# Three 256-column matmuls per weight tile in place of a 512- and a 256-column one, in the MLP up projection of a two-layer decoder trunk

## The chip, the cores and the metric

The kernel runs on one core of a Trainium2 chip. The metric is device microseconds of one execution. Before the change three runs gave 2304.35, 2304.24 and 2301.83 us, median 2304.24 us. The profile shown here is of one further execution, which took 2303.22 us.

## The reference, cut to what matters

The trunk has two layers over 256 tokens of width 2048. Each layer normalises, runs an attention mixer, adds it back, normalises again and runs a squared-ReLU MLP of inner width 8192:

```python
D_MODEL = 2048; SEQ = 256; D_FF = 4 * D_MODEL

def sq_relu_mlp(h, w_up, w_down):
    return jnp.square(jax.nn.relu(h @ w_up)) @ w_down

def reference(x, ...):
    h = x
    for layer in range(DEPTH):            # DEPTH = 2
        hn = rms_norm(h, ln_mix_g[layer])
        h = h + mixer(hn, ...)            # layer 0: forgetting + dilated heads, layer 1: sparse attention
        hn = rms_norm(h, ln_mlp_g[layer])
        h = h + sq_relu_mlp(hn, w_mlp_up[layer], w_mlp_down[layer])
    return h
```

The change concerns `h @ w_up` and the squared ReLU behind it.

## The kernel before, in words

**Precision.** Each fp32 operand is kept as two fp32r parts, a high part and the rest (low part). A product is the sum of three partial products: high by high, high by low, low by high. The activations lie transposed in `xT[:, k, part]`: 16 slices k of 128 input columns, and for each slice 256 token columns of the high part (part 0), then 256 of the low part (part 1), next to each other.

**Weights.** SP streams weight pieces of 1 MB from HBM into three `raw` buffers (L227). Half a piece is a unit: 128 by 1024 numbers, that is two k-slices of 512 weight columns. ScalarE copies a unit into one of four `wh` buffers (high part, L235), VectorE subtracts to get `wl` (low part, L236). This `split` is issued three units ahead of the unit's matmuls (L264).

**Two kinds of matmul units.** `a_units` (the projections, the out projections and the MLP down projection) stream the weights: a 128-token slice of the activations is the stationary operand, 512 weight columns move; each partial product is one 512-column matmul (L298 to L300 in a group's first and last unit, L311 in the units between, where successive matmuls alternate between two PSUM banks). `b_units` (the MLP up projection only) stream the activations: a 128-column slice j of the weights is stationary. For each k and each j of 4 there are two matmuls: the high weights against the 512 columns [high part | low part] (L340), and the low weights against the 256 columns of the high part (L337), which add into the first half of the same bank. So one PSUM bank holds one j: its left half high-high plus low-high, its right half high-low.

**Order.** In the first and the last unit of a group the order is one j after the other; in the units between, it goes through the four j for one k-slice and then for the other, each low matmul one step behind (L351 to L357). All matmuls load their own stationary operand (a LDWEIGHTS each, `PEld` in the profile), also where two in a row have the same one, as L298 and L299.

**MLP.** The inner width is done in 8 blocks of 1024 columns; `up_units(b)` makes block b in two groups g of 512 columns (8 units each), `down_units(b)` consumes it. The order is up(0), up(1), down(0), up(2), down(1), ..., up(7), down(6), down(7). A group g of the up projection uses four PSUM banks: bank 3 and banks 0 to 2 for g = 0, banks 4 to 7 for g = 1; the down projection uses banks 2n and 2n+1 for its four column groups n.

**Evacuation.** When a j is done in the last unit, `evac` issues a ScalarE copy of the right half to SBUF (L767), a VectorE add of the left half (L768), and a VectorE (max 0) times itself (L769); a background task then makes the high part on ScalarE (L773) and the low part on VectorE (L774), both into `big`. Background tasks (`bg`) are issued in slots: each `yield` of a unit's generator gives one slot (L265, L266), and `bg.need` issues a task at once if it isn't done. Instructions of each engine run in the order issued.

Of the kernel before, what the change touches and what calls it, by code (L numbers as in the profile page):

```python
# [12 lines left out]
AF = mybir.ActivationFunctionType  # L13
ALU = mybir.AluOpType
AX = mybir.AxisListType

S = 256
# [130 lines left out]
def trunk_kernel(ctx: ExitStack, tc: tile.TileContext, x, w_up, w_down, even_w_in, even_w_out,  # L148
                 odd_w_in, odd_w_out, k_w1, k_w2, v_w1, v_w2, vec, rows, con, rot_in, ident_in, out):
    nc = tc.nc  # L150
# [4 lines left out]
    def sb(name, shape, dt=F32):  # L155
        return pool.tile(shape, dt, name=name)

    bank = [psum.tile([128, 512], F32, name=f"bank{i}") for i in range(8)]
# [5 lines left out]
    xT = sb("xT", [128, KT, 2, S], F32R)  # L164
# [5 lines left out]
    T = [sb(f"t{i}", [128, 1024]) for i in range(10)]  # L170
# [26 lines left out]
    bg = Background()  # L197
# [9 lines left out]
    def weight_chunk(w, k0, nk, segs):  # L207

        width = sum(n for _, n in segs)
        pieces, at = [], 0  # L210
        for c0, n in segs:
            src = w[k0 * 128:(k0 + nk) * 128, c0:c0 + n].rearrange("(k p) c -> p k c", p=128)
            pieces.append((nk, width, at, n, src))
            at += n
        return chunk(pieces)
# [101 lines left out]
    def b_units(w, c0, rhs, evac, banks, pre=None):  # L317


        state = {}  # L320
        for i0 in range(0, KT, 4):
            ci = weight_chunk(w, i0, 4, [(c0, 512)])
            for j0 in (0, 2):
                ks = [i0 + j0, i0 + j0 + 1]

                def gen(u, ks=ks):
                    first, last = ks[0] == 0, ks[-1] == KT - 1
                    if pre:
                        pre(ks)
                    if first:  # L330
                        state["banks"] = banks()
                    h = wh[u % NHL].rearrange("p (k c) -> p k c", c=512)
                    lo = wl[u % NHL].rearrange("p (k c) -> p k c", c=512)
                    def part(j, n, lo_part):
                        o, k = state["banks"][j], ks[n]
                        if lo_part:
                            nc.tensor.matmul(o[:, :S], lo[:, n, j * 128:(j + 1) * 128], rhs(k)[:, :S], start=False,  # L337
                                             stop=last and n == 1)
                        else:
                            nc.tensor.matmul(o, h[:, n, j * 128:(j + 1) * 128], rhs(k), start=first and n == 0, stop=False)  # L340

                    if first or last:
                        for j in range(4):
                            for n in range(2):
                                part(j, n, 0)
                                part(j, n, 1)
                            if last:
                                evac(j, state["banks"][j])
                            yield
                    else:  # L350
                        steps = [(j, n) for n in range(2) for j in range(4)]  # L351
                        for i, (j, n) in enumerate(steps):
                            part(j, n, 0)
                            if i:
                                part(*steps[i - 1], 1)
                            if i == 7:
                                part(j, n, 1)  # L357
                            if i % 2:
                                yield

                units.append((ci, j0 * 512, 1024, gen, True))

    def t_units(w, c0, m, rhs, evac, pre):
# [87 lines left out]

    def xr(k):
        return xT[:, k].rearrange("p a t -> p (a t)")

    rot = {"main": 0, "tp": 0, "s": 0, "sq": 0}

    def rotate(name, of):
        rot[name] += 1
        return of[(rot[name] - 1) % len(of)]
# [4 lines left out]
    class Prep:  # L464
# [7 lines left out]
        def evac(self, hf, ps):  # L472
            r = self.norm.rows()
            if hf == 0 and self.src.name in owner:
                bg.need(owner[self.src.name])
            q = self.src[:, hf * 512:(hf + 1) * 512]
            sq = SQ[hf]
            nc.scalar.activation(q, ps, AF.Copy, scale=r[:, hf:hf + 1])
            nc.scalar.activation(sq, ps, AF.Square, scale=r[:, 2 + hf:3 + hf])
            nc.vector.tensor_reduce(self.ms[:, hf * 4:hf * 4 + 4], sq.rearrange("p (h d) -> p h d", h=4), AX.X, ALU.add)  # L480
            if hf == 1:
                self.task = owner[self.src.name] = bg.spawn(self.rest(), 2)

        def rest(self):
            ms = self.ms
            nc.vector.tensor_scalar(ms, ms, EPS, None, op0=ALU.add)
            nc.gpsimd.tensor_tensor(ms, ms, nhalf, ALU.pow)
            yield 4, "d"
            for hf in range(2):
                q = self.src[:, hf * 512:(hf + 1) * 512].rearrange("p (h d) -> p h d", h=4)  # L490
                f = ms[:, hf * 4:hf * 4 + 4, None].to_broadcast([128, 4, HD])
                nc.vector.tensor_tensor(q, q, f, ALU.mult)
                if self.rope is not None:
                    rope(q, self.rope[0][:, hf], self.rope[1][:, hf], 128)
                if hf == 0:
                    yield 3, "d"
            yield 8
            yield (self.free or (lambda: True)), "t"
            yield from self.turn()
# [127 lines left out]
    heads = {}  # L627
# [65 lines left out]
    for kind, base, h0 in (("fox", 0, 0), ("dil", 4 * FOX_W + 8, 8)):  # L693
        for blk in range(2):
# [16 lines left out]
            if nblk == 1:  # L711
                t_units(W, 4 * FOX_W, 8, xr, evac_fa, n0.need)
# [40 lines left out]
    def mlp(layer, norm, nxt):  # L753
        up, down = w_up[layer], w_down[layer]
        NBLK = DFF // 1024

        def hid(b):
            return big[:, (b % 2) * 8:(b % 2) * 8 + 8]

        def up_units(b):  # L760
            for g in range(2):
                def evac(j, ps, g=g):
                    k = g * 4 + j
                    t, s_, q_ = T[j][:, 0:S], T[j][:, S:2 * S], T[j][:, 2 * S:3 * S]
                    if ("hid", j) in heads:
                        bg.need(heads["hid", j])
                    nc.scalar.activation(t, ps[:, S:], AF.Copy)  # L767
                    nc.vector.tensor_tensor(s_, ps[:, :S], t, ALU.add)  # L768
                    nc.vector.scalar_tensor_tensor(q_, s_, 0.0, s_, op0=ALU.max, op1=ALU.mult)  # L769

                    def rest():
                        d = hid(b)
                        nc.scalar.activation(d[:, k, 0], q_, AF.Copy)  # L773
                        nc.vector.tensor_tensor(d[:, k, 1], q_, d[:, k, 0], ALU.subtract)  # L774
                        yield 2
                    heads["hid", j] = bg.spawn(rest(), 1 + j)
                b_units(up, b * 1024 + g * 512, xr, evac, lambda g=g: bank[4:8] if g else [bank[3]] + [rotate("main", bank[0:3]) for _ in range(3)], norm.need)

        def down_units(b):
            for n in range(NB):  # L780
                bks = (bank[2 * n], bank[2 * n + 1])

                def evac(hf, ps, n=n):
                    if n == 0 and hf == 0 and b == 0:
                        bg.need(norm.rtask)
                    xd = xs[:, hf, n * 512:(n + 1) * 512]
                    nc.vector.scalar_tensor_tensor(xd, ps, norm.r2[:, hf:hf + 1], xd, op0=ALU.mult, op1=ALU.add)  # L787
                    if b < NBLK - 1:
                        return
                    if nxt is not None:  # L790
                        nxt.square(n, hf)
                        if hf == 1:
                            m = 2 * ((n + 3) % 4)
                            nxt.start(n, (bank[m], bank[m + 1]), 4)
                            if n == NB - 1:
                                nxt.rtask = bg.spawn(stats(nxt), 4)
                    else:
                        nc.sync.dma_start(out[hf * 128:(hf + 1) * 128, n * 512:(n + 1) * 512], xd)

                a_units(down, [(n * 512, 512)],  # L800
                        lambda k, part, hf: hid(b)[:, k - 8 * b, part, hf * 128:(hf + 1) * 128],
                        list(range(8 * b, 8 * b + 8)), evac, lambda bks=bks: bks,
                        lambda ks: bg.need(*[heads["hid", j] for j in range(4)]))

        for b in range(NBLK):
            up_units(b)
            if b:
                down_units(b - 1)
        down_units(NBLK - 1)

    def even_ready(ks):
# [287 lines left out]
```

## Time and profile before

| | |
|---|---|
| median of three runs | 2304.24 us (2301.83 to 2304.35) |
| profiled execution, its own time | 2303.22 us |
| its span, first to last instruction | 2301.4 us |
| PE busy | 2285.3 us (99%), 11399 matmuls |
| VectorE busy | 1382.1 us (60%) |
| ScalarE busy | 1086.6 us (47%) |
| granted TensorE clock, mean | 0.999 |
| HBM traffic over the span | 179 GB/s |

How to read it: matmuls are pipelined, so a matmul's own duration is longer than the time until the next one starts; the spacing of starts is what adds up to the span. "Releaser" is what ended an engine's wait. L311 means line 311 of the kernel before; `bank<-xT,wh` names the output, the moving operand and the stationary operand in this order for matmuls. Idle time of an engine that is not the bound costs nothing.

### The profile page before, as it was taken

What the parts mean: (1) busy time and instruction counts of PE and PEld (TensorE: products, weight loads), DVE (VectorE), ACT (ScalarE), POOL (GpSimd) and SP (SyncE); (2) the same over time, 40 slices, a digit from 0 to 9 for tenths busy, and PEclk for the clock granted to TensorE, in tenths of its full rate; (3) what the DMA queues carried; (4) which work ended last, traced back from release to release, by engine and by line L of the source; (5) the groups of instructions that cost most, each with busy time, mean ns of one, the idle gap of its engine ahead of it and who ended that gap; (6) DMA issues with size and microseconds to landing.
All of it is one profiled execution on the core that took longest, in us unless ns stands there. A gap on an engine that the chain in (4) does not pass through costs nothing.

```text
span 2301.4 us, 28635 instructions
## 1 busy us (share of the span) xinstructions
PE 2285.3 (99%) x11399; PEld 1922.5 (84%) x11399; DVE 1382.1 (60%) x2075; ACT 1086.6 (47%) x1573; POOL 30.0 (1%) x28
## 2 busy tenths in 40 slices
PE   8999999999999999999999999999999999999999
PEld 6788888888888888888888888788888888888887
DVE  5565655666566566566654666766666556566564
ACT  5554554544444444444443555555544444444342
POOL 0000000000000000000000000000000000000000
PEclk9999999999999999999999999999999999999999
DMA  6555555555555565565546653335555565555654
GB/s 240 165 165 171 176 165 167 181 192 193 184 198 186 188 196 183 183 201 184 188 148 204 215 165 121 118 110 174 191 186 190 181 199 193 187 193 176 203 195 148
DMA packets 212694, 414.47 MB, mean 180 GB/s; under 512 B 10705, under 2 KB 11985, under 8 KB 212561
## 3 DMA queue, kind: packets, MB, share of 16 engines
q1 hardware_dynamic: 211552, 411.53, 54.9%
q8 instruction: 89, 1.46, 0.3%
q10 hardware_dynamic: 1008, 1.12, 0.1%
q14 instruction: 45, 0.36, 0.0%
HBM read 410.52 MB, written 2.10 MB: 179 GB/s over the span
## 4 chain that ended last, share of the span: by engine, by line
PE 96%; DVE 1%; ACT 1%; DMA 1%; issue 0%; POOL 0%; ACTq 0%; POOLq 0%
PE bank L311 34%; PE bank L340 21%; PE bank L337 11%; PE bank L300 8%; PE bank L298 8%; PE bank L299 8%; PE bank L616 1%; PE bank L588 1%; PE bank L611 1%; DMA raw<-in_even_w_in 1%; PE bank L876 1%; DVE wl L236 1%; PE bank L507 1%; PE bank L617 0%; PE bank L425 0%; PE bank L584 0%
## 5 line engine op out<-in xcount | busy, mean ns | idle before, releaser
L236 DVE TENSOR_TENSOR wl<-raw,wh 128x1024 fp32r<-128x1024 f32 (+1 forms) x772 | 937.9, 1219 | 768.5 <-ACT wh L235 766.3
L235 ACT ACTIVATE wh<-raw 128x1024 fp32r<-128x1024 f32 (+1 forms) x772 | 812.3, 1054 | 864.8 <-PE bank L311 324.1
L340 PE MATMUL bank<-xT,wh 128*128 128x512 f32 x2048 | 707.6, 397 | 0.0
L337 PE MATMUL bank<-xT,wl 128*128 128x256 f32 x2048 | 543.0, 281 | 0.0
L340 PEld LDWEIGHTS bank<-xT,wh 128*128 128x128 f32 x2048 | 371.5, 188 | 75.2
L337 PEld LDWEIGHTS bank<-xT,wl 128*128 128x128 f32 x2048 | 386.6, 189 | 18.5
L311 PE MATMUL bank<-wh,big 128*128 128x512 f32 x1280 | 358.8, 391 | 0.0
L311 PE MATMUL bank<-wh,xT 128*128 128x512 f32 x1156 | 325.6, 395 | 0.8 <-ACT xT L430 0.7
L311 PEld LDWEIGHTS bank<-wh,big 128*128 128x128 f32 x1280 | 239.6, 188 | 49.3 <-DVE big L625 0.2
L298 PE MATMUL bank<-wh,big 128*128 128x512 f32 x640 | 252.8, 395 | 0.0
L311 PEld LDWEIGHTS bank<-wh,xT 128*128 128x128 f32 x1156 | 214.9, 188 | 44.6 <-ACT xT L430 1.3
L300 PE MATMUL bank<-wh,big 128*128 128x512 f32 x640 | 249.5, 390 | 0.0
L299 PE MATMUL bank<-wl,big 128*128 128x512 f32 x640 | 249.2, 389 | 0.0
L311 PE MATMUL bank<-wl,big 128*128 128x512 f32 x640 | 202.8, 393 | 0.0
L311 PE MATMUL bank<-wl,xT 128*128 128x512 f32 x578 | 188.5, 397 | 0.0
L300 PEld LDWEIGHTS bank<-wh,big 128*128 128x128 f32 x640 | 120.1, 188 | 25.7 <-DVE big L625 0.4
L298 PEld LDWEIGHTS bank<-wh,big 128*128 128x128 f32 x640 | 120.4, 188 | 24.4 <-ACT big L624 0.2
L311 PEld LDWEIGHTS bank<-wl,big 128*128 128x128 f32 x640 | 120.2, 188 | 24.5
L299 PEld LDWEIGHTS bank<-wl,big 128*128 128x128 f32 x640 | 120.4, 188 | 23.5
L311 PEld LDWEIGHTS bank<-wl,xT 128*128 128x128 f32 x578 | 108.5, 188 | 22.5 <-DVE wl L236 0.2
L787 DVE SCALAR_TENSOR_TENSOR xs<-bank,r_m,xs 128x512 f32<-128x512 f32 x128 | 89.9, 743 | 7.8 <-PE bank L300 7.8
L773 ACT ACTIVATE big<-t 128x256 fp32r<-128x256 f32 x128 | 52.5, 415 | 81.9 <-DVE t L769 81.9
(179 smaller groups left out, 1454.9 us busy)
## 6 DMA issues: line engine op xcount, KB each, us to landing
raw<-in_w_up SPq DMA_DIRECT2D x128, 1024.0 KB, 5.3
raw<-in_w_down SPq DMA_DIRECT2D x128, 1024.0 KB, 5.1
raw<-in_even_w_in SPq DMA_DIRECT2D x55, 1024.0 KB, 5.1
raw<-in_odd_w_in SPq DMA_DIRECT2D x40, 1024.0 KB, 5.1
raw<-in_even_w_out SPq DMA_DIRECT2D x16, 1024.0 KB, 5.0
raw<-in_odd_w_out SPq DMA_DIRECT2D x16, 1024.0 KB, 5.3
out_x<-xs SPq DMA_DIRECT2D x8, 256.0 KB, 2.5
xs<-in_x SPq DMA_DIRECT2D x3, 512.0 KB, 8.8
```

Of the source, the lines that this page charges most:

```text
L235: nc.scalar.activation(h, r, AF.Copy)
L236: nc.vector.tensor_tensor(lo, r, h, ALU.subtract)
L298: nc.tensor.matmul(o, lhs(k, 0, hf), h[:, n], start=st, stop=False)
L299: nc.tensor.matmul(o, lhs(k, 0, hf), lo[:, n], start=False, stop=False)
L300: nc.tensor.matmul(o, lhs(k, 1, hf), h[:, n], start=False, stop=last and n == len(ks) - 1)
L311: nc.tensor.matmul(bks[hf], lhs(k, part, hf), w_[:, n], start=False, stop=False)
L337: nc.tensor.matmul(o[:, :S], lo[:, n, j * 128:(j + 1) * 128], rhs(k)[:, :S], start=False, stop=last and n == 1)
L340: nc.tensor.matmul(o, h[:, n, j * 128:(j + 1) * 128], rhs(k), start=first and n == 0, stop=False)
L507: nc.tensor.transpose(b[:, i * S + hf * 128:i * S + hf * 128 + 128], self.src[:, hf * 512 + h * 128:hf * 512 + (h + 1) * 128], ident)
L588: nc.tensor.matmul(s[:, 128:384], qT[:, 128:256], kT, start=True, stop=bias is None, skip_group_check=True)
L773: nc.scalar.activation(d[:, k, 0], q_, AF.Copy)
L787: nc.vector.scalar_tensor_tensor(xd, ps, norm.r2[:, hf:hf + 1], xd, op0=ALU.mult, op1=ALU.add)
```

## The change

In `b_units` the 512-column matmul and the 256-column one become three 256-column matmuls that add into the same 256 PSUM columns: high weights by high activations, high weights by low activations, low weights by high activations. Two j share one bank, so a group needs two banks (4 and 5 for g = 0, 6 and 7 for g = 1). All units go one j after the other; there are four yields per unit as before. The evacuation handles two j at a time: ScalarE takes the ReLU of 512 columns straight from PSUM, VectorE squares it, and the background task makes high and low parts of 512 columns. A helper `xr2(k, part)` gives one part of a slice.

```diff
-                    def part(j, n, lo_part):
-                        o, k = state["banks"][j], ks[n]
-                        if lo_part:
-                            nc.tensor.matmul(o[:, :S], lo[:, n, j * 128:(j + 1) * 128], rhs(k)[:, :S], start=False,
-                                             stop=last and n == 1)
-                        else:
-                            nc.tensor.matmul(o, h[:, n, j * 128:(j + 1) * 128], rhs(k), start=first and n == 0, stop=False)
...
+                    for j in range(4):
+                        o = state["banks"][j // 2][:, (j % 2) * S:(j % 2 + 1) * S]
+                        for n, k in enumerate(ks):
+                            hj, lj = h[:, n, j * 128:(j + 1) * 128], lo[:, n, j * 128:(j + 1) * 128]
+
+                            nc.tensor.matmul(o, hj, rhs(k, 0), start=first and n == 0 and j % 2 == 0, stop=False,
+                                             skip_group_check=True)
+                            nc.tensor.matmul(o, hj, rhs(k, 1), start=False, stop=False, skip_group_check=True)
+                            nc.tensor.matmul(o, lj, rhs(k, 0), start=False, stop=last and n == 1, skip_group_check=True)
+                        if last and j % 2:
+                            evac(j // 2, state["banks"][j // 2])
+                        yield
...
-                def evac(j, ps, g=g):
-                    k = g * 4 + j
-                    t, s_, q_ = T[j][:, 0:S], T[j][:, S:2 * S], T[j][:, 2 * S:3 * S]
...
-                    nc.scalar.activation(t, ps[:, S:], AF.Copy)
-                    nc.vector.tensor_tensor(s_, ps[:, :S], t, ALU.add)
-                    nc.vector.scalar_tensor_tensor(q_, s_, 0.0, s_, op0=ALU.max, op1=ALU.mult)
+                def evac(m, ps, g=g):
+                    k, t = g * 4 + 2 * m, T[2 * (g % 2) + m]
+                    r_, q_ = t[:, 0:2 * S], t[:, 2 * S:4 * S]
...
+                    nc.scalar.activation(r_, ps, AF.Relu)
+                    nc.vector.tensor_tensor(q_, r_, r_, ALU.mult)
...
-                        nc.scalar.activation(d[:, k, 0], q_, AF.Copy)
-                        nc.vector.tensor_tensor(d[:, k, 1], q_, d[:, k, 0], ALU.subtract)
+                        d, q2 = hid(b)[:, k:k + 2], q_.rearrange("p (k t) -> p k t", k=2)
+                        nc.scalar.activation(d[:, :, 0], q2, AF.Copy)
+                        nc.vector.tensor_tensor(d[:, :, 1], q2, d[:, :, 0], ALU.subtract)
...
-                b_units(up, b * 1024 + g * 512, xr, evac, lambda g=g: bank[4:8] if g else [bank[3]] + [rotate("main", bank[0:3]) for _ in range(3)], norm.need)
+                b_units(up, b * 1024 + g * 512, xr2, evac, lambda g=g: bank[4 + 2 * g:6 + 2 * g], norm.need)
```

## Rows read from the trace of the kernel before

**Rows 1.** The page's busy time by engine, and the granted clock in 40 slices.
```profile
PE 2285.3 (99%) x11399; PEld 1922.5 (84%) x11399; DVE 1382.1 (60%) x2075; ACT 1086.6 (47%) x1573; POOL 30.0 (1%) x28
...
PEclk9999999999999999999999999999999999999999
```

**Rows 2.** All waits of PE: line waited for, us in total, times, longest us.
```profile
PE bank L425 <- DMA xs<-in_x: 5.4, 2, 4.5
PE bank L985 <- DVE big L625: 2.3, 1, 2.3
...
PE bank L298 <- DVE xT L431: 1.0, 2, 0.8
```

**Rows 3.** Busy time by stretch: one up group, the next down block; us, engines, clock, DMA.
```profile
883.47:906.01 22.54, 22.54 (x130) 19.61 (x129) 14.01 (x21) 10.89 (x16) 0.00 (x0) 1.00 0.57 188
906.01:949.54 43.53, 43.53 (x194) 36.05 (x193) 27.54 (x34) 19.12 (x23) 0.00 (x0) 1.00 0.58 190
```

**Rows 4.** The page's costliest groups: busy us, mean ns of one, idle before.
```profile
L340 PE MATMUL bank<-xT,wh 128*128 128x512 f32 x2048 | 707.6, 397 | 0.0
L337 PE MATMUL bank<-xT,wl 128*128 128x256 f32 x2048 | 543.0, 281 | 0.0
...
L299 PEld LDWEIGHTS bank<-wl,big 128*128 128x128 f32 x640 | 120.4, 188 | 23.5
```

**Rows 5.** Chain of waits: shares of the span by line; pieces at 643 and 1256 us.
```profile
by line: PE bank L311 34.3%; PE bank L340 20.8%; PE bank L337 10.5%; PE bank L300 8.0%; PE bank L298 8.0%; PE bank L299 8.0%; PE bank L616 0.9%; PE bank L588 0.8%; PE bank L611 0.7%; DMA raw<-in_even_w_in 0.7%; PE bank L876 0.6%; DVE wl L23
...
643.11 5.44 PE bank L311 x24
...
1256.26 7.12 PE bank L876 x64
```

**Rows 6.** Timeline of PE, first unit of a group from 506.68 us: start, us, instruction.
```profile
506.68 0.40 PE L340 MATMUL bank<-xT,wh 128*128 128x512 f32 x1
506.91 0.28 PE L337 MATMUL bank<-xT,wl 128*128 128x256 f32 x1
...
509.45 0.40 PE L340 MATMUL bank<-xT,wh 128*128 128x512 f32 x1
```

**Rows 7.** The same view, first unit of the group from 883.47 us.
```profile
883.82 0.40 PE L340 MATMUL bank<-xT,wh 128*128 128x512 f32 x1
...
885.94 0.40 PE L340 MATMUL bank<-xT,wh 128*128 128x512 f32 x1
```

**Rows 8.** The same view, two low matmuls in a row at a unit's end.
```profile
899.88 0.40 PE L340 MATMUL bank<-xT,wh 128*128 128x512 f32 x1
900.12 0.40 PE L337 MATMUL bank<-xT,wl 128*128 128x256 f32 x2
900.36 0.63 PE L340 MATMUL bank<-xT,wh 128*128 128x512 f32 x2
900.83 0.28 PE L337 MATMUL bank<-xT,wl 128*128 128x256 f32 x1
```

**Rows 9.** The same view, short fp32r matmuls in the attention of layer 0.
```profile
92.80 0.33 PE L593 MATMUL bank<-triu,nlf 128*128 128x128 f32 x2
92.96 0.46 PE L298 MATMUL bank<-wh,xT 128*128 128x512 f32 x1
```

**Rows 10.** ScalarE groups, by shape: busy us, mean ns of one, idle before.
```profile
L773 ACT ACTIVATE big<-t 128x256 fp32r<-128x256 f32 x128 | 52.5, 415 | 81.9 <-DVE t L769 81.9
L767 ACT ACTIVATE t<-bank 128x256 f32<-128x256 f32 x128 | 43.8, 368 | 0.0
...
L511 ACT ACTIVATE t<-bank 128x512 f32<-128x512 f32 x8 | 4.5, 594 | 4.5 <-PE bank L507 4.4
...
L235 ACT ACTIVATE wh<-raw 128x512 fp32r<-128x512 f32 x4 | 2.3, 620 | 0.0
```

**Rows 11.** VectorE groups, by shape.
```profile
L769 DVE SCALAR_TENSOR_TENSOR t<-t 128x256 f32<-128x256 f32 x128 | 54.4, 425 | 4.4
L768 DVE TENSOR_TENSOR t<-bank,t 128x256 f32<-128x256 f32 x128 | 53.5, 418 | 0.0
L774 DVE TENSOR_TENSOR big<-t,big 128x256 fp32r<-128x256 f32 x128 | 51.1, 420 | 15.5 <-ACT big L773 15.5
...
L492 DVE TENSOR_TENSOR t<-t,ms 128x512 f32<-128x512 f32 x28 | 19.1, 686 | 3.0 <-POOL ms L487 3.0
...
L236 DVE TENSOR_TENSOR wl<-raw,wh 128x512 fp32r<-128x512 f32 x4 | 2.6, 688 | 0.1
```

More of the change, by code (lines that the diff above doesn't have):

```diff
@@ L333, in gen @@
                     lo = wl[u % NHL].rearrange("p (k c) -> p k c", c=512)
-                    def part(j, n, lo_part):
-                        o, k = state["banks"][j], ks[n]
-                        if lo_part:
-                            nc.tensor.matmul(o[:, :S], lo[:, n, j * 128:(j + 1) * 128], rhs(k)[:, :S], start=False,
-                                             stop=last and n == 1)
-                        else:
-                            nc.tensor.matmul(o, h[:, n, j * 128:(j + 1) * 128], rhs(k), start=first and n == 0, stop=False)
[L342 to L359, printed above, removed]
+                    for j in range(4):
[9 more added lines that the diff above has]
+                        yield
                 units.append((ci, j0 * 512, 1024, gen, True))
@@ L453, in xr, with xr2 @@
         return xT[:, k].rearrange("p a t -> p (a t)")
+    def xr2(k, part):
+        return xT[:, k, part]
     rot = {"main": 0, "tp": 0, "s": 0, "sq": 0}
@@ L761, in up_units @@
             for g in range(2):
-                def evac(j, ps, g=g):
-                    k = g * 4 + j
-                    t, s_, q_ = T[j][:, 0:S], T[j][:, S:2 * S], T[j][:, 2 * S:3 * S]
-                    if ("hid", j) in heads:
-                        bg.need(heads["hid", j])
-                    nc.scalar.activation(t, ps[:, S:], AF.Copy)
-                    nc.vector.tensor_tensor(s_, ps[:, :S], t, ALU.add)
-                    nc.vector.scalar_tensor_tensor(q_, s_, 0.0, s_, op0=ALU.max, op1=ALU.mult)
+                def evac(m, ps, g=g):
+                    k, t = g * 4 + 2 * m, T[2 * (g % 2) + m]
+                    r_, q_ = t[:, 0:2 * S], t[:, 2 * S:4 * S]
+                    if ("hid", m) in heads:
+                        bg.need(heads["hid", m])
+                    nc.scalar.activation(r_, ps, AF.Relu)
+                    nc.vector.tensor_tensor(q_, r_, r_, ALU.mult)
                     def rest():
-                        d = hid(b)
-                        nc.scalar.activation(d[:, k, 0], q_, AF.Copy)
-                        nc.vector.tensor_tensor(d[:, k, 1], q_, d[:, k, 0], ALU.subtract)
+                        d, q2 = hid(b)[:, k:k + 2], q_.rearrange("p (k t) -> p k t", k=2)
+                        nc.scalar.activation(d[:, :, 0], q2, AF.Copy)
+                        nc.vector.tensor_tensor(d[:, :, 1], q2, d[:, :, 0], ALU.subtract)
                         yield 2
-                    heads["hid", j] = bg.spawn(rest(), 1 + j)
-                b_units(up, b * 1024 + g * 512, xr, evac, lambda g=g: bank[4:8] if g else [bank[3]] + [rotate("main", bank[0:3]) for _ in range(3)], norm.need)
+                    heads["hid", m] = bg.spawn(rest(), 1 + m)
+                b_units(up, b * 1024 + g * 512, xr2, evac, lambda g=g: bank[4 + 2 * g:6 + 2 * g], norm.need)
         def down_units(b):
@@ L802, in down_units @@
                         list(range(8 * b, 8 * b + 8)), evac, lambda bks=bks: bks,
-                        lambda ks: bg.need(*[heads["hid", j] for j in range(4)]))
+                        lambda ks: bg.need(*[heads["hid", j] for j in range(2)]))
         for b in range(NBLK):
```

## The prediction

> **What bounds the kernel now.** I began with the page's busy times: PE is busy 99% of the span, and the granted clock is 9 in every slice, 1.00 in the stretches looked at below, so TensorE runs at its upper level (2.4 GHz) throughout [rows 1, 3]. VectorE (60%) and ScalarE (47%) have room. Busy is no proof for a pipelined engine, so I next read what PE waits for. The longest entry is 5.4 us, in the start-up; the list's entries come to about 12 us in all, and neither line of the up projection (L337, L340) stands in it [rows 2]. Then the busy time by stretch: in one group of the up projection PE is busy 22.54 of 22.54 us, VectorE 14.01, ScalarE 10.89, DMA 0.57 [rows 3]. The chain of waits gives L340 and L337 together 31.3% of the span, 720 us, all of it on the path that sets the end [rows 5]. So the stage that is changed is bound by how closely its matmuls follow each other, and by nothing else. What must be predicted is one number, the spacing of 256-column matmuls in an unbroken row, and it is a small difference of large terms.
>
> **Spacings that the trace shows.** The durations in the list of costliest groups (397 and 281 ns) overlap [rows 4]; starts must be used.
> - 512 columns only: 24 in 5.44 us, 226.7 ns each [rows 5]. At 2.4 GHz and a column a cycle 512 columns are 213.3 ns (an estimate from the granted clock), so 13.4 ns come on top.
> - A pair of the up projection (512 and 256 columns): 64 in 22.54 us, 352 ns [rows 3]; the chain's 720.3 us over 2048 pairs give 351.7 [rows 4, 5]. I use 352.0. The columns alone are 320.0, so 32.0 come on top, 16.0 per matmul.
> - It isn't the same everywhere. One unit of eight pairs takes 509.45 - 506.68 = 2.77 us, 346 ns a pair [rows 6]; six pairs in another take 885.94 - 883.82 = 2.12 us, 353 ns [rows 7]. The first is 226.7 + 120: just what a pair costs if every matmul, long or short, has 13.4 ns on top. Both units run strictly one j after the other into one bank, as the new code always does, so that order by itself costs at most a few ns.
> - Two 256-column matmuls in a row occur at a unit's end: 900.36 - 900.12 = 0.24 us, 120 ns each at this view's resolution of 10 ns [rows 8].
>
> **The change, part by part.**
>
> *Matmuls.* Per pair one 512 and one 256 go, three 256 come: 2048 more matmuls and as many weight loads. The columns stay at 768. If each matmul carries a fixed cost c, the triple takes 320 + 3c. With c = 13.3 ns that is 3 x 120.0 = 360.0, +8.0 ns per pair, x 2048 = +16.4 us. With the up projection's present c of 16.0 it is 368.0, +16.0 ns, +32.8 us. The bound on the other side is a cost that goes with the columns: at the rate of the 512-column row a 256 takes 113.3, a triple 340.0, -12.0 ns, -24.6 us. At the pair's own rate, 352.0/3 = 117.3, it is no change. I take c = 13.3: it is what the only stream of one width in the trace shows, steadily, and 120 is also what the nearest row, two 256s in a row, shows. The sum's pivot is thus 117.3 ns per 256-column matmul; each ns above or below moves the time by 6.1 us.
>
> The Trainium skill ("TensorE: Matmul & The Clock Gate", section "Back-to-back issue gap") gives N/2.4 + 2.5 ns for the spacing when warm. That would be 215.8 for 512 columns, and the trace shows 226.7, so it does not hold for these operands as it stands; by it the triple costs 2.5 ns more than the pair, an estimate of +5.1 us.
>
> *Weight loads and issue.* Three loads instead of two per 768 columns, the high weights twice in a row. Loads are not shared between neighbours with the same stationary operand: L299, whose operand is that of L298 just before, has its own 640 loads [rows 4]. Can a load and an issue fit beside 256 columns? 64 fp32 matmuls with a load each follow at 7.12/64 = 111 ns [rows 5], and two 128-column fp32r matmuls took 92.96 - 92.80 = 0.16 us, 80 each [rows 9]; both are below 113. So I cost it at nothing beyond c; if it doesn't fit, the third rival has the price.
>
> *Evacuation.* Per group before: ScalarE 4 x (368 + 415) = 3.1 us, VectorE 4 x (418 + 425 + 420) = 5.1 us [rows 10, 11]. After: ScalarE twice a 512-column ReLU from PSUM (the nearest row, a copy of 512 from PSUM, 594) and a 512-column copy to fp32r (620): 2.4 us; VectorE twice a product of 512 (686) and a difference to fp32r (688): 2.7 us [rows 10, 11]. That takes 0.7 us from ScalarE and 2.3 us from VectorE per group, 22 and 74 us in all, beside a PE that waits for neither [rows 2, 3]: worth nothing. It could be worth at most the 1.0 us that PE waits for VectorE at the norms [rows 2]. The first evacuation starts one j later (some 0.7 us), and its result is first read by a down block which comes after another whole block (43.5 us [rows 3]), or after the next up groups.
>
> *Banks.* Two banks per group. g = 0 now takes banks 4 and 5, whose last readers are the down projection's third column group, ended one column group (a quarter of 43.5 us) earlier, or, at the start of an MLP, the norm's transposes of the third quarter, with the out projection's last column group in between. g = 1 takes 6 and 7, 22.5 us after their last evacuation. No new wait; bound: the 1.0 us above, once more per layer.
>
> *Order, slots, queues.* Four yields per unit stay, so background work is issued at the same rate; fewer tasks (two per group instead of four). SP's loads, POOL's work and the splits three units ahead keep their places. 4096 more PE instructions are fetched; DMA is at 0.57 in the stage [rows 3].
>
> **Sum.** The profiled execution took 2303.22 us, 1.8 us of it around its span; +16.4 gives 2319.6. The median of the runs lies 1.0 us above the profiled one: 2320.6.
>
> **The rivals.**
>
> 1. *The cost goes with the columns at the pair's present rate.* Then 117.3 per matmul and 2304 us. For it: 256-column matmuls in the mixed stream are followed after 0.11 to 0.12 us, 512s after 0.23 to 0.24 [rows 6 to 8], near the ratio of their columns. Against it: single starts jitter by about 0.01 us between like instructions, as large as what is in dispute. The page's 2.5 ns would set this case at 2309; the row for 512 speaks against that rule's size, not against its form, a small fixed part.
>
> 2. *Faster: the short matmuls run at the clean rate.* If the extra 12 ns of a pair (352.0 against 1.5 x 226.7 = 340.0) come from mixing lengths, a stream of one length loses them: 113.3 each, 340.0, -24.6 us, 2279.7. For it: the stream of 512s runs at 226.7 without jitter, the mixed one doesn't. Against: even the best unit shows 346, not 340 [rows 6], and the pair in a row shows 120 [rows 8]. It decides once a 256-column matmul in the new stream takes under 116.6 ns.
>
> 3. *The weight load beside 256 columns is too long.* If the 12 ns are paid by each matmul whose weights load beside 256 columns, a pair pays once, a triple three times: 3 x (113.3 + 12.0) = 376.0, +24.0 ns, +49.2 us, 2353.4. If the second load of the same high weights were free after all, twice: 364.0, 2328.8. For it: 113 ns is close to the 111 of [rows 5]. Against: the 80 ns of [rows 9]. The Trainium skill (the same page, section "LDWEIGHTS (loading the stationary operand)") puts a load at columns/1.2, an estimate of 107 ns for 128 columns; no run here shows a load by itself, its 188 ns record overlaps the matmuls [rows 4].
>
> **How the numbers follow.** Fixed cost per matmul 0.46 (2316 to 2340, its point 2320.6), cost by columns 0.22 (2300 to 2309), clean rate 0.17 (2276 to 2296), weight load 0.15 (2340 to 2360). The range 2294 to 2356 leaves out most of the clean rate and the top of the last. A change below 0.2% (4.6 us) is what a measurement of this kernel can't tell from none; 0.2% is 0.75 ns on each 256-column matmul. Faster: the clean rate and a little of the second case, 0.19. Same: the rest of the second case, 0.20. Slower: 0.61.
>
> **What would show it.** In the new profile: PE still without waits in the up projection; a group of 192 matmuls taking 23.0 us (360 x 64) against 22.54; the three 256-column lines spaced 120 ns on average; the down blocks still 226.7 ns a matmul and 43.5 us; VectorE's busy time down by about 74 us and ScalarE's by 22. A group of 22.5 us means the cost goes with columns, 21.8 the clean rate, 24.1 the weight load. The prediction is wrong in its basis if PE shows waits for PSUM banks, `wl` or `big` in the MLP, or if the down blocks change.

## The result, and the profile after

The changed kernel takes 2319.86 us (median of 4 runs, 2319.45 to 2320.69) against 2303.98 us for the kernel before (4 runs): 1.0071 times as long, 95% interval 1.0059 to 1.0083, 15.9 us more. It is slower. The prediction said 2320.6 us, slower, with 16.4 us more.

The page of the kernel after answers to [rows 1]: PE stays at 99%, with 2048 more matmuls and loads; VectorE and ScalarE have less to do, and the clock is 9 in every slice. Numbers are busy us, share of the span, and count.

```profile
span 2317.7 us, 32381 instructions
PE 2300.6 (99%) x13447; PEld 2031.6 (88%) x13447; DVE 1326.7 (57%) x1819; ACT 1078.6 (47%) x1445; POOL 30.0 (1%) x28
...
PEclk9999999999999999999999999999999999999999
...
L339 PE MATMUL bank<-xT,wh 128*128 128x256 f32 x2048 | 579.8, 283 | 0.0
L342 PE MATMUL bank<-xT,wl 128*128 128x256 f32 x2048 | 579.6, 283 | 0.0
L341 PE MATMUL bank<-xT,wh 128*128 128x256 f32 x2048 | 579.6, 283 | 0.0
```

L339 and L341 are the high weights by the high and the low activations, L342 the low weights by the high activations. The busy time by stretch answers to [rows 3]: one up group, then a down block (us; busy of PE, PEld, VectorE, ScalarE, POOL; clock; DMA share; GB/s).

```profile
800.52:823.56 23.04, 23.04 (x195) 23.04 (x193) 12.30 (x13) 10.64 (x12) 0.00 (x0) 1.00 0.56 186
823.56:867.11 43.55, 43.55 (x195) 36.04 (x194) 25.80 (x27) 18.55 (x19) 0.00 (x0) 1.00 0.58 188
```

The group took 22.54 us and takes 23.04 us: 0.50 us more. There are 32 groups, so this comes to 16.0 us, where the times differ by 15.9 us and the spans of the two profiles by 16.3 us (2317.7 against 2301.4). The down block is the same within 0.02 us. The list of PE's waits, which answers to [rows 2], still holds no line of the up projection:

```profile
PE bank L411 <- DMA xs<-in_x: 5.4, 2, 4.1
PE bank L973 <- DVE big L614: 2.3, 1, 2.3
PE bank L298 <- DVE xT L417: 1.6, 2, 1.4
```

And the timeline of PE shows what the group consists of: starts 0.12 us apart, from the first matmul of a block of two groups to the first of the down block behind it.

```profile
777.49 0.28 PE L339 MATMUL bank<-xT,wh 128*128 128x256 f32 x1
777.60 0.28 PE L341 MATMUL bank<-xT,wh 128*128 128x256 f32 x1
777.72 0.28 PE L342 MATMUL bank<-xT,wl 128*128 128x256 f32 x1
...
823.44 0.28 PE L342 MATMUL bank<-xT,wl 128*128 128x256 f32 x1
823.56 0.40 PE L298 MATMUL bank<-wh,big 128*128 128x512 f32 x1
```

384 matmuls lie between 777.49 and 823.56: 46.07 us, 120.0 ns each, 359.9 per triple. In the kernel before the same two groups took 45.07 us (817.41 - 772.34), 352.1 per pair:

```profile
772.34 0.39 PE L340 MATMUL bank<-xT,wh 128*128 128x512 f32 x1
...
817.41 0.40 PE L298 MATMUL bank<-wh,big 128*128 128x512 f32 x1
```

### The profile page after: what moved, and what is told of

Read it like the earlier page. It is cut to its first block, busy times and chain, and to the rows that moved or that the text cites. A ratio compares the mean times of both kernels' runs of the same rounds, so it can differ in the third digit from the quotient of the medians.

```text
span 2317.7 us, 32381 instructions
## 1 busy us (share of the span) xinstructions
PE 2300.6 (99%) x13447; PEld 2031.6 (88%) x13447; DVE 1326.7 (57%) x1819; ACT 1078.6 (47%) x1445; POOL 30.0 (1%) x28
## 4 chain that ended last, share of the span: by engine, by line
PE 96%; DVE 1%; DMA 1%; ACT 1%; issue 0%; POOL 0%; ACTq 0%; POOLq 0%
PE bank L311 34%; PE bank L342 11%; PE bank L341 11%; PE bank L339 11%; PE bank L300 8%; PE bank L298 8%; PE bank L299 8%; PE bank L605 1%; PE bank L577 1%; DMA raw<-in_even_w_in 1%; PE bank L600 1%; PE bank L864 1%; DVE wl L236 1%; PE bank L496 1%; PE bank L411 0%; PE bank L606 0%
## 5 line engine op out<-in xcount | busy, mean ns | idle before, releaser
L339 PE MATMUL bank<-xT,wh 128*128 128x256 f32 x2048 | 579.8, 283 | 0.0
L342 PE MATMUL bank<-xT,wl 128*128 128x256 f32 x2048 | 579.6, 283 | 0.0
L341 PE MATMUL bank<-xT,wh 128*128 128x256 f32 x2048 | 579.6, 283 | 0.0
L341 PEld LDWEIGHTS bank<-xT,wh 128*128 128x128 f32 x2048 | 393.1, 192 | 0.5
L339 PEld LDWEIGHTS bank<-xT,wh 128*128 128x128 f32 x2048 | 393.1, 192 | 0.5
L342 PEld LDWEIGHTS bank<-xT,wl 128*128 128x128 f32 x2048 | 393.1, 192 | 0.0
L299 PE MATMUL bank<-wl,big 128*128 128x512 f32 x640 | 249.3, 390 | 0.0
L299 PEld LDWEIGHTS bank<-wl,big 128*128 128x128 f32 x640 | 120.3, 188 | 23.4
```

The source lines that it names most:

```text
L299: nc.tensor.matmul(o, lhs(k, 0, hf), lo[:, n], start=False, stop=False)
L339: nc.tensor.matmul(o, hj, rhs(k, 0), start=first and n == 0 and j % 2 == 0, stop=False, skip_group_check=True)
L341: nc.tensor.matmul(o, hj, rhs(k, 1), start=False, stop=False, skip_group_check=True)
L342: nc.tensor.matmul(o, lj, rhs(k, 0), start=False, stop=last and n == 1, skip_group_check=True)
```

## The experiments

The spacing of 120.0 ns left three questions: is the 13.3 ns on top of the columns a fixed price of each matmul, the time of its weight load, or a rate; what made the pair before cost 5.3 ns more than 226.7 + 120.0; and was anything else in the change worth time? Experiments marked "one run" have one time each, beside one run of the kernel before on the same chip; their verdict is the spacing of starts in the trace, most often over hundreds of like matmuls. The granted clock was 0.997 to 1.000 in every run. Spacings said to be read to the nanosecond are from the stored trace, which is finer than the views printed here. In the code cuts, `...` and `[...]` stand for what is left out.

**Fewer moving columns** (one run each).

```diff
-  nc.tensor.matmul(o, hj, rhs(k, 0), ...)           # and the other two alike
+  W_ = S if first and n == 0 else 192               # 128 in the second experiment
+  nc.tensor.matmul(o[:, :W_], hj, rhs(k, 0)[:, :W_], ...)
```

> The changed kernel with its three matmuls cut to 192 columns (64 token columns of each product are left out), except for the first k-slice of a group. Theory 1, a fixed 13.3 ns on top of columns/2.4 for every matmul: spacing 80.0 + 13.3 = 93.3 ns; 5760 of the 6144 matmuls are cut, 26.7 ns each, 154 us less than 2319.9: 2166 us, unless the splits or the weight stream become late. Theory 2, 120 ns is the floor of a matmul with a 128-column weight load: the spacing stays at 112 to 120 ns, 2274 to 2320 us. Theory 3, a cost by columns at 120/256: 90.0 ns, 2147 us.

> The same with 128 columns (half of the token columns left out). Theory 1: 53.3 + 13.3 = 66.7 ns between matmuls where PE isn't waiting; at this pace a group would take 13 us, and the weight stream (4 MB a group, over 300 GB/s) or VectorE's splits could hold it, so the spacing inside a unit is what counts. Theory 2: 112 to 120 ns, 2274 to 2320 us. Theory 3: 60.0 ns.

Measured: 2272.09 us with 192 columns and 2272.02 with 128, the kernel before at 2301.36 beside them. The two rows of each timeline below are the first matmul of two groups and the first of the down block behind them; 384 matmuls lie between.

```profile
765.36 0.28 PE L340 MATMUL bank<-xT,wh 128*128 128x256 f32 x1
...
808.38 0.41 PE L298 MATMUL bank<-wh,big 128*128 128x512 f32 x1
```

```profile
765.16 0.28 PE L340 MATMUL bank<-xT,wh 128*128 128x256 f32 x1
...
808.13 0.45 PE L298 MATMUL bank<-wh,big 128*128 128x512 f32 x1
```

43.02/384 = 112.0 ns with 192 columns, 42.97/384 = 111.9 ns with 128. Theory 1 (93.3 and 66.7) and theory 3 fail below 256 columns; there is a floor, as theory 2 has it, and it lies at 112, not at 120. So at 256 columns the floor is 8 ns away and does not bind by itself.

**Two matmuls of 384 columns** in place of 512 and 256 (one run).

```diff
-  nc.tensor.matmul(o[:, :S], lo[...], rhs(k)[:, :S], ...)
+  nc.tensor.matmul(o[:, :384], lo[...], rhs(k)[:, :384], ...)
-  nc.tensor.matmul(o, h[...], rhs(k), ...)
+  w_ = 512 if first and n == 0 else 384
+  nc.tensor.matmul(o[:, :w_], h[...], rhs(k)[:, :w_], ...)
```

> The kernel before, with both matmuls of a pair 384 columns wide (half of the high-by-low product left out, and columns of low-by-low work added that the result doesn't ask for): the same 768 columns in two matmuls of one width. Theory 1: 160.0 + 13.3 = 173.3 ns each, 346.7 a pair against 352.0, some 10.5 us under the kernel before: 2293 us. Theory 3 at the rate of 120/256: 180 ns, 360 a pair, some 16 us over it; at the rate of the 512-column stream (226.7/512): 170.0 ns, 24 us under it.

Measured: 2301.02 us against 2301.36 beside it. Where only 384s follow each other, 22 of them start between these rows:

```profile
799.05 0.33 PE L337 MATMUL bank<-xT,wl 128*128 128x384 f32 x1
...
802.86 0.33 PE L337 MATMUL bank<-xT,wl 128*128 128x384 f32 x1
```

3.81/22 = 173.2 ns: theory 1's 173.3, not 170.0 and not 180. The time did not follow the expectation, because that forgot its own exception: the first k-slice of a group keeps the 512 columns, 128 more in each of 128 matmuls, 53.3 ns x 128 = 6.8 us, and there the lengths alternate. To the nanosecond, the first unit of a group takes 3.05 us and the others 2.77, so the exception costs some 8.8 us in all, and two groups take 44.92 us against 45.07. That is 2.4 us less over the kernel, no more than runs of one kernel differ.

**Fewer weight columns** (one run each): 64, then 32, of the 128 in the up projection.

```diff
+  M_ = 128 if first and n == 0 else 64              # 32 in the second experiment
+  nc.tensor.matmul(o[:M_], hj[:, :M_], rhs(k, 0), ...)   # and the other two alike
```

> The changed kernel with only 64 of the 128 weight columns loaded and multiplied, except for the first k-slice of a group (half of the inner width is left out of the sums). Theory 1: the cost is the matmul's own, 120 ns stay, 2319.9 us. Theory 2: the load of 64 columns is half as long, so the spacing falls to what 256 columns need, 107 to 113 ns: 40 to 77 us less, 2243 to 2280 us.

> The changed kernel with 32 of the 128 weight columns loaded and multiplied in the up projection, except for the first k-slice of a group (three quarters of the inner width are left out of the sums). Theory A: 106.7 + 3.3 = 110.0 ns a matmul where 64 columns gave 113.7: 2258 to 2262 us. If the cost comes in steps, or 113 is the floor of a matmul of 256 columns: 113 ns, 2280 us.

Measured: 2280.94 us (before: 2301.36) with 64 columns and 2282.66 (before: 2303.13) with 32. Again 384 matmuls lie between the rows, 64 columns first.

```profile
767.86 0.28 PE L340 MATMUL bank<-xT,wh 128*128 128x256 f32 x1
...
811.56 0.40 PE L298 MATMUL bank<-wh,big 128*128 128x512 f32 x1
```

```profile
767.42 0.28 PE L340 MATMUL bank<-xT,wh 128*128 128x256 f32 x1
...
811.15 0.40 PE L298 MATMUL bank<-wh,big 128*128 128x512 f32 x1
```

43.70/384 = 113.8 and 43.73/384 = 113.9 ns; in the units without the excepted k-slice both are 113.3, to the nanosecond. So some 6.7 of the 13.3 ns hang on having more than 64 weight columns, and the rest does not get smaller with them: not theory 1 (120), and not a price per loaded column either. Fewer weight columns also mean fewer rows of output; no run separates the two.

**The same for 512 moving columns**: 64 stationary columns in the middle units of all `a_units` (one run).

```diff
-  nc.tensor.matmul(bks[hf], lhs(k, part, hf), w_[:, n], start=False, stop=False)
+  nc.tensor.matmul(bks[hf][:64], lhs(k, part, hf)[:, :64], w_[:, n], start=False, stop=False)
```

> The changed kernel with only 64 of the 128 stationary columns loaded and multiplied in the middle units of the projections and the down projection (line 311; half of the tokens get an incomplete sum there). Theory A, the cost on top of the columns belongs to the weight load (13.3 ns per 128 loaded columns, 6.7 per 64): the 512-column stream goes from 226.7 to 220.0 ns, 3654 matmuls, 24 us less: 2296 us. Theory B, a load of 64 columns only matters beside short matmuls, where 128 columns do not fit: 226.7 ns stays, 2320 us.

Measured: 2328.59 us (before: 2303.13 beside it), 8.7 us more than the changed kernel, where one expectation was 24 us less and the other no change. 24 matmuls lie between these rows of its timeline:

```profile
738.88 0.63 PE L311 MATMUL bank<-wh,big 128*64 128x512 f32 x2
...
744.40 0.39 PE L298 MATMUL bank<-wh,big 128*128 128x512 f32 x1
```

5.52/24 = 230.0 ns against 226.7 with the full load [rows 5]. Theory A falls. Beside long matmuls a smaller load gains nothing: it costs 3.3 ns here and, by the 8.7 us, 2.4 ns on average over the 3654 matmuls.

**128 moving and 64 loaded columns** (one run; both edits from above together).

> The changed kernel with 128 moving columns (in place of 256) and 64 loaded columns, except for the first k-slice of a group. With 128 loaded columns both 128 and 192 moving columns gave 112 ns. If that floor is the time of the load, it is half as long: the stream then needs 53.3 + 6.7 = 60 ns and PE becomes limited by the splits or the weight stream (below 2200 us). If it is the issue of a load and a matmul: 112 ns and 2272 us again.

Measured: 2013.93 us (before: 2303.13). Where PE doesn't wait, the narrow matmuls start 60 ns apart (36 of them in 2.16 us between the rows below, in the middle of a group); at this pace the splits are late now and then.

```profile
708.89 0.22 PE L341 MATMUL bank<-xT,wh 128*64 128x128 f32 x1
...
711.05 0.22 PE L341 MATMUL bank<-xT,wh 128*64 128x128 f32 x1
```

Its list of PE's waits (us, times, longest):

```profile
PE bank L344 <- DVE wl L236: 13.2, 23, 0.9
```

A load and a matmul can thus be issued every 60 ns, so the floor of 112 ns is not their issue; it hangs on having 128 weight columns, and the time of their load is the plain reading. The Trainium skill ("TensorE: Matmul & The Clock Gate", section "LDWEIGHTS (loading the stationary operand)") has columns/1.2 for a load, an estimate of 106.7 ns for 128. The measured floor lies 5 ns above that.

**The pair before, with 64 weight columns** (one run; `[:, :64]` on the stationary operands, as above, in the kernel before).

> The kernel before (512- and 256-column pairs) with 64 of the 128 weight columns, except for the first k-slice and the last low matmul of a group. Theory A: 320 + 2 x 6.7 = 333.3 ns a pair plus what mixing the lengths costs (5.3 with full loads). If the mixing cost hangs on the load, it is gone: 333 ns, 38 us less than before, 2265 us. If it doesn't: 338.7 ns, 27 us less, 2276 us.

Measured: 2290.71 us against 2303.13, 12.4 us less. 128 pairs lie between these rows:

```profile
770.13 0.39 PE L342 MATMUL bank<-xT,wh 128*128 128x512 f32 x1
...
814.43 0.40 PE L298 MATMUL bank<-wh,big 128*128 128x512 f32 x1
```

44.30/128 = 346.1 ns a pair: neither 333 nor 338.7. The gain of 6.0 ns is about what the short matmul alone gained above. Some surplus is left: the single spacings with half the load, 230.0 and 113.8, add up to 343.8.

**The order of the pair** (ten runs each, in the kernel before): strictly one j after the other in all units; and all eight 512-column matmuls of a unit before its eight 256-column ones.

```diff
+  for j in range(4):                      # old_strict
+      for n in range(2):
+          part(j, n, 0)
+          part(j, n, 1)
...                                        # evac in the last unit, yield
+  for n in range(2):                      # old_grouped
+      for j in range(4):
+          part(j, n, 0)
+      yield
+  for j in range(4):
+      for n in range(2):
+          part(j, n, 1)
...                                        # evac in the last unit, yield
```

> The kernel before with one j after the other in all units (the changed kernel's order) and its matmuls and evacuation as before. If the order is worth nothing: 2304 us within 0.2%. The strict units of the kernel before take 346 to 354 ns a pair against 352 in the others, so the bounds are 11 us less and 4 us more.

> The kernel before with the eight 512-column matmuls of a unit first and its eight 256-column ones after them, all else as before. Theory 1 with mixing as the source of the rest (352.0 against 226.7 + 120.0 = 346.7 a pair): the 512s at 226.7, the 256s at 120.0, 5.3 ns less per pair, 10.9 us less: 2293 us, 0.5% faster than the kernel before. If the rest isn't due to the alternation of lengths: 2304 us.

Measured: strict 2306.31 us, 1.0016 of the kernel before (1.0007 to 1.0026); grouped 2298.24 us, 0.9982 (0.9973 to 0.9992), against 2302.86. The strict order takes 45.21 us for two groups, 353.2 a pair:

```profile
773.99 0.39 PE L340 MATMUL bank<-xT,wh 128*128 128x512 f32 x1
...
819.20 0.40 PE L298 MATMUL bank<-wh,big 128*128 128x512 f32 x1
```

The grouped order shows its rows of eight in the timeline:

```profile
772.33 1.98 PE L340 MATMUL bank<-xT,wh 128*128 128x512 f32 x8
774.15 1.12 PE L337 MATMUL bank<-xT,wl 128*128 128x256 f32 x8
775.10 2.00 PE L340 MATMUL bank<-xT,wh 128*128 128x512 f32 x8
776.94 1.12 PE L337 MATMUL bank<-xT,wl 128*128 128x256 f32 x8
```

The first eight 512s, which come after other 512s, take 774.15 - 772.33 = 1.82 us, 227 ns each; the next eight, after 256s, 776.94 - 775.10 = 1.84 us, 230 each; the 256s 0.95 us, 119 each. So a change from short to long costs some 20 to 30 ns, spread over the first long ones, where the mixed order pays 5.3 ns on average in each of eight pairs. Grouping gives back under half of what was expected (4.6 of 10.9 us), and it is the fastest version here that does the whole work, faster than both kernels.

These 256s also answer a rival that no run was made for, that several matmuls in a row into the same PSUM columns are what costs: here the output changes bank after every second matmul, and they start 119 ns apart, 120 to the nanosecond once the row is under way.

**The same weights twice in a row**, undone (four runs): the low weights' matmul between the two of the high weights.

> The changed kernel with the low weights' matmul between the two of the high weights, so that no two matmuls in a row have the same stationary operand. Theory 1: 120 ns, no change. If a repeated load of the same weights is cheaper than a new one, it is slower: by up to 13.3 ns per triple, 27 us.

Measured: 2320.31 us, 1.0076 of the kernel before (1.0061 to 1.0091): as the changed kernel. In this stream a repeated load is as dear as a new one.

**More VectorE work** (four runs).

```diff
-  nc.vector.tensor_tensor(q_, r_, r_, ALU.mult)
+  for _ in range(4):
+      nc.vector.tensor_tensor(q_, r_, r_, ALU.mult)
```

> The changed kernel with each product of the evacuation on VectorE done four times instead of once: 3 x 64 more instructions of about 686 ns, some 130 us more of VectorE work, more than the change took from it. If the evacuation is hidden beside PE, as the prediction has it: no change, 2319.9 us within 0.2%. If VectorE's work reaches the end of the chain: up to 130 us more.

Measured: 2319.93 us (2318.87 to 2320.56), 1.0076 (1.0059 to 1.0092) of the kernel before, with VectorE busy 120 us longer than in the changed kernel:

```profile
PE 2300.4 (99%) x13447; PEld 2031.3 (88%) x13447; DVE 1447.0 (62%) x2011; ACT 1070.9 (46%) x1445; POOL 30.0 (1%) x28
```

The evacuation is hidden beside PE, and 120 us more of it cost nothing; so the saving there can hardly be worth anything.

## Why the prediction was right, point by point

**The bound.** PE paces the up projection with no wait, before and after, and 120 us more of VectorE work leave the time alone. That the 55 us less of the change are worth nothing follows from the groups: their 16.0 us leave no room for a gain elsewhere.

**The term that carries the sum.** 320 + 3 x 13.3 = 360.0 ns was forecast for a triple, 359.9 is measured; +8.0 ns x 2048 = +16.4 us against +15.9. The choice of 13.3 over 16.0, the mean of the up projection before, was the step that could have gone wrong, and the runs show why 13.3 was the one to take: uniform streams of 256, 384 and 512 columns with full loads start 120.0, 173.2 and 226.7 ns apart, columns/2.4 + 13.3 in each case. The surplus to 16.0 goes with mixing the lengths, which the change ends: in the kernel before, grouping the lengths recovers part of it.

**Where it was lucky.** One of the two supports for 120 did not hold. In the view, which resolves 10 ns, the two 256s in a row of [rows 8] take 0.24 us. To the nanosecond they take 116 and 119 ns, 235 together, and 116.3 and 119.3 on average over the 192 such places. Over the whole kernel before, a 256 is followed after 117 ns and a 512 after 235, on average: the ratio of rival 1, and its 117.3. So the trace of the kernel before spoke for 13.3 by its row of 512s alone; that it holds for 256s was shown by the runs only.

**What the surplus hangs on is open.** Mixing is not enough to cause it: the strict unit of [rows 6] alternates the lengths and takes 346.6 ns a pair to the nanosecond, without any surplus. So do, within 1 ns, the other strict units of the first two blocks of each layer's MLP that run unbroken; the strict units of the later blocks take 351 to 354. Nothing that was tried tells them apart.

**What "a fixed cost of a matmul" got wrong.** With 128 loaded columns the form holds from 256 columns up; below, 112 ns is the floor. With 64 loaded columns the part on top is 6.7 ns at 128 and at 256 moving columns (60.0 and 113.3), but 16.7 at 512 (230.0); with 32 it is 6.7 still at 256. So the 13.3 ns are no property of the matmul alone, and not a fixed price per loaded column either. What makes them up stays open; the number was right for streams with full loads, like the one it was read from.

**Rival 1, cost by columns** (117.3): out by the 120.0 of the changed kernel. **Rival 2, the clean rate** (113.3): that rate exists, but only where 64 weight columns or fewer are loaded; with full loads, ending the mixture of lengths did not bring it. **Rival 3, the load too long beside 256 columns**: its price of 125.3 ns did not come, since 112 < 120; but the load is nearer than the prediction thought. It took the 80 ns of [rows 9] as a sign of room. That row is no steady stream. The weight loads of the same moment, which the prediction did not show, start earlier and 0.11 to 0.12 us apart (92.91 - 92.68 = 0.23 us for two), so the 80 ns are not the pace of a load and a matmul:

```profile
92.68 0.30 PEld L593 LDWEIGHTS bank<-triu,nlf 128*128 128x128 f32 x2
92.91 0.19 PEld L298 LDWEIGHTS bank<-wh,xT 128*128 128x128 f32 x1
```

The 111 ns of [rows 5] were the better sign: the floor measured 112. The room at 256 columns is 8 ns, not 40.

**Weight loads are not shared**: the row of L299 was read rightly; the order without repeats is neither faster nor slower.

**The evacuation's size.** Row by row it came as worked out: the three VectorE groups of [rows 11] (159.0 us) became two of 44.1 and 43.8, 71 us less against 74 forecast, and ScalarE's two (96.3 us) became two of 40.5 and 37.7, 18 less against 22. These are the groups after (busy us, mean ns, idle before):

```profile
L761 ACT ACTIVATE big<-t 128x512 fp32r<-128x512 f32 x64 | 40.5, 632 | 25.4 <-DVE t L757 25.4
L756 ACT ACTIVATE t<-bank 128x512 f32<-128x512 f32 x64 | 37.7, 590 | 16.1 <-PE bank L342 16.1
```

```profile
L762 DVE TENSOR_TENSOR big<-t,big 128x512 fp32r<-128x512 f32 x64 | 44.1, 689 | 22.3 <-ACT big L761 22.3
L757 DVE TENSOR_TENSOR t<-t 128x512 f32<-128x512 f32 x64 | 43.8, 685 | 0.0
```

The engines' busy totals fell by less, 55.4 and 8.0 us; the prediction's "busy time down by about 74 and 22" was too large for the totals. The totals count time in which two records of an engine overlap only once. Added up record by record, the trace has 1459.7 us of VectorE before and 1386.7 after, 73 less, and 1155.8 and 1134.1 of ScalarE, 22 less: the forecast was right for the records, and overlap hid part of it in the totals.

**Banks and order.** Two banks per group added no wait on PE that the lists show. The wait at the norms is 1.6 us against 1.0, but the grouped order, which keeps four banks, has it too:

```profile
PE bank L298 <- DVE xT L424: 1.6, 2, 1.4
```

The strict order in itself costs the old pair 1.1 ns (353.2 against 352.1) and 3.4 us. In a uniform stream it costs nothing: in the run with 384 columns the strict last unit of a group takes 346.6 ns a pair, as the units between do.

## What to carry to other kernels

Where PE runs without waits, price a change of matmul shapes by the spacing of starts in a long steady stream of one shape, not by two rows at a view's resolution, not by the durations of the records and not by the mean of a mixed stream. The same columns in more matmuls cost the part on top once more for each (13.3 ns here, with full loads and 256 columns or more), and work saved on engines that PE doesn't wait for pays for none of it. If two lengths are needed, run them in rows of their own: here that alone took 0.2% off the kernel before.

## What the runs showed of the hardware that was not expected

- Starts in a steady stream of these fp32r matmuls, 128 loaded columns: 112 ns for 128 and 192 moving columns, 120.0 for 256, 173.2 for 384, 226.7 for 512. Halving 256 moving columns saves only 8 ns.
- Loading fewer columns is not always cheaper: 256 moving columns go from 120.0 to 113.3 with 64 loaded and stay there with 32, while 512 moving columns go up from 226.7 to 230.0.
- Mixing 512 and 256 columns costs 5.3 ns a pair on average over the sum of the uniform spacings (352 against 346.7), but nothing in some units (346.6). With half the load a pair takes 346.1, against 230.0 + 113.8 = 343.8; the 230.0 is from another stage.
